# Between the layers: one weight tile's split on ScalarE and GpSimd, the next tile's split and the second block's transposes later in the order

## The chip, the cores and the metric

One core of a Trainium2 chip runs the whole program. The metric is the device time of one execution in microseconds (us), the median of several runs. A profiled execution of the kernel before gives the trace. In the text PE is TensorE (the matrix engine), DVE is VectorE, ACT is ScalarE, POOL is GpSimd and SP is the engine that issues most DMAs.

## The reference

A two-layer decoder trunk on x of 512 tokens by 1024 (float32). Layer 0 mixes tokens with native sparse attention (NSA), layer 1 with differential attention; each layer has a norm before and one after.

```python
def rmsnorm(x, g):
    y = xf * lax.rsqrt(jnp.mean(xf * xf, axis=-1, keepdims=True) + EPS)
    return (y * g.astype(jnp.float32)).astype(x.dtype)
...
    for i in range(DEPTH):                       # DEPTH = 2
        u = rmsnorm(x, norm_pre[i])
        y = nsa_mixer(u, ...) if i % 2 == 0 else diff_mixer(u, ...)   # each begins with u @ w_in, ends with o @ w_out
        x = x + rmsnorm(y, norm_post[i])
...
def diff_mixer(u, table, w_in, ...):
    q, k, v, z = jnp.split(u @ w_in, 4, axis=-1)
```

This case is about the seam: the end of `o @ w_out` of layer 0, its post-norm and the residual, the pre-norm of layer 1, and the first columns of `u @ w_in` of layer 1 (those of v).

## The kernel before, in words

Every product of a weight and an activation is made of three matmuls. Both operands are cut into a rounded part (`h`, type fp32r) and the rest (`l`), and PE adds h·h, l·h and h·l into one PSUM bank. So each weight tile of 128x1024 that a DMA brings has to be *split* before PE can use it (`Stream.split`): for each of four pieces of 128x256 one instruction writes `h` (a copy that rounds, line 158/159 or 165) and one writes `l = raw - h` (a subtraction, line 160 or 167). By default POOL does both. A table can name the engines for a tile: `"PD"` is POOL for the copy and DVE for the subtraction, `"AP"` is ACT for the copy and POOL for the subtraction.

The weight tiles form one stream, in the order in which jobs use them. A job is a set of output columns. The jobs at the seam are `o1` (columns 512 to 1023 of layer 0's output projection; 24 matmuls of 128x512 for each of the four blocks of 128 tokens, line 467), then `dv0` and `dv1` (256 columns each of layer 1's v; 24 matmuls of 128x256 a block and job, line 218). Split tiles stand in three slots `whi`/`wlo` and, at the seam alone, in six slots `wx`. `o1` has one tile in `whi`/`wlo` and three in `wx`; `dv0` has two in `whi`/`wlo`; the first tile of `dv1` stands in `wx` (it takes slots that `o1` gives up), its second in `whi`/`wlo`. DMAs fill two raw tiles `wraw` ahead of the splits.

When `o1` is done with a token block t, this chain runs for that block:

- `y_evac`: ACT squares the PSUM bank and sums (line 453), DVE multiplies it by the post-norm weight into `bigC` (line 454);
- `yend`: ACT takes a square root (line 345), DVE finishes the scale (lines 346 to 352) and writes the new x into `bigD` (line 1052, two halves of 128x512);
- `after0`: ACT issues a DMA of the block to DRAM, and `prenorm` begins: ACT squares both halves (line 361), POOL multiplies both by the pre-norm weight into `bigC` (line 364), DVE and ACT make the scale (lines 335, 345 to 349), DVE scales `bigC` (line 369);
- `turn` (called `p0` to `p3` here for the four blocks): PE transposes the block in eight matmuls (line 380), ACT copies the result as `h` into `bigF` (line 100), DVE writes `l` into `bigE` (line 105). Then `dv0` and `dv1` can use the block.

`dv0` writes block 0 and block 1 into the same PSUM bank, one half each. The second half's first matmul waits until ACT has copied the first half out (line 571). `a0` to `a3` below are the four blocks of `dv0`, `b0` to `b3` those of the first tile of `dv1`.

PE's order at the seam is the order of the code (`manual_schedule`); the list `SEQ` sets it behind `o1`. The order on the other engines comes from a list scheduler which works with its own estimates of durations; `tc.issue_after(i)` makes what is traced inside the block stand behind instruction i where they are on the same engine. The lines that matter most:

```python
            h, l = (T["wx"].tile([128, 1024], F32R, name="wx", tag="wx", bufs=6) for _ in range(2))
...
                if i in self.by:
                    eh, el = self.by[i][a // cuts]
...
    ws.by[jobs[index['dv1']].first] = SPD
```

Of the kernel before, what the change touches and what calls it, by code (L numbers as in the profile page):

```python
# [15 lines left out]
OP = mybir.AluOpType  # L16
# [2 lines left out]
S = 512  # L19
WARM = 7  # L20
EARLY = True
PRE1 = 29
ZE = 'gpsimd', 'vector'
OB = (2,2,2)
LAG = 1
# [14 lines left out]
OPRE = 0  # L40
ODELAY = 0
QN = 1
SPD = ('PD',)*4
SEQ = 'a0 a1 p2 b0 b1 a2 p3 b2 a3 b3'.split()
PRE = {16: 2, 24: 3}
SPX = ('AP',) * 4
SPN = 2
# [21 lines left out]
def trunk(ctx: ExitStack, tc: tile.TileContext, x, table, npre, npost, w_in, pe_k, w1_k, w2_k,  # L69
          pe_v, w1_v, w2_v, w_out, dw_in, lq1, lk1, lq2, lk2, subln, dw_out, steps, out):  # L70
    nc = tc.nc
# [9 lines left out]
    def bank(tag):  # L81
        return ps.tile([128, 512], F32, name=tag, tag=tag, bufs={"mm": 2, "S": 2, "T": 3, "av": 1}[tag])

    def slot(tag, shape, dt=F32):
        return big.tile(shape, dt, name="big" + tag, tag="big" + tag)
# [4 lines left out]
    def pttile(dt=F32R):  # L90
        return work.tile([128, 512], dt, name="PT", tag="PT", bufs=NPT)

    def small(n, dt=F32, tag="st", bufs=8):
        return work.tile([128, n], dt, name=tag, tag=tag, bufs=bufs)
# [4 lines left out]
    def hi(dst, src, scale=1.0):  # L99
        return nc.scalar.activation(dst, src, AF.Copy, scale=scale)  # L100
# [3 lines left out]
    def lo(dst, src, h):  # L104
        nc.vector.tensor_tensor(dst, src, h.bitcast(F32), op=OP.subtract)  # L105
# [67 lines left out]
    T = {}  # L173
# [113 lines left out]
    run = Runner()  # L287
# [43 lines left out]
    def part_sum(ss, m=EPS):  # L331

        m0 = small(1, tag="m0", bufs=6)
        if isinstance(m, float):
            nc.vector.tensor_scalar(m0, ss, 1.0 / D, m, op0=OP.mult, op1=OP.add)
        else:
            nc.vector.scalar_tensor_tensor(m0, ss, 1.0 / D, m, op0=OP.mult, op1=OP.add)
        return m0

    def row_rstd(m0, ss, split=False):  # L340

        r = small(1, tag="rstd")
        m = small(1, tag="rs1")
        q = small(1, tag="rs3")
        T0["a"] = nc.scalar.activation(r, ss, AF.Sqrt, scale=1.0 / D, bias=m0).ins
        nc.vector.scalar_tensor_tensor(m, ss, 1.0 / D, m0, op0=OP.mult, op1=OP.add)
        nc.vector.reciprocal(r, r)
        nc.vector.scalar_tensor_tensor(q, r, m, r, op0=OP.mult, op1=OP.mult)
        nc.vector.tensor_scalar(q, q, -0.5, 1.5, op0=OP.mult, op1=OP.add)
        if split:  # L350
            return r, q
        nc.vector.tensor_tensor(r, r, q, op=OP.mult)
        return r

    def prenorm(t, src, xn, grow, uh, ul, early):

        halves = (slice(0, 512), slice(512, 1024))
        ss = [small(1, tag="ss") for _ in range(2)]
        with tc.issue_after(T0["a"]) if "a" in T0 else ExitStack():
            for c, s in zip(halves, ss):  # L360
                nc.scalar.activation(pttile(F32) if early else xn[:, c], src[:, c], AF.Square, accum_out=s)
        if early:
            for c, g in zip(halves, grow):
                nc.gpsimd.tensor_tensor(xn[:, c], src[:, c], g, op=OP.mult)
        m0 = part_sum(ss[0])
        if early:
            r, q = row_rstd(m0, ss[1], split=True)
            for c in halves:
                nc.vector.tensor_scalar(xn[:, c], xn[:, c], r, q, op0=OP.mult, op1=OP.mult)
        else:  # L370
            r = row_rstd(m0, ss[1])
            for c, g in zip(halves, grow):
                nc.vector.scalar_tensor_tensor(xn[:, c], src[:, c], r, g, op0=OP.mult, op1=OP.mult)

        def turn():
            for i in range(2):
                p = bank("T")
                for j in range(4):
                    k = i * 4 + j
                    nc.tensor.transpose(p[:, j * 128:(j + 1) * 128], xn[:, k * 128:(k + 1) * 128], ident)  # L380
                pv = p.rearrange("p (j c) -> p j c", j=4)
                cs = slice(t * 128, (t + 1) * 128)
                x = hi(uh[:, i * 4:i * 4 + 4, cs], pv).ins
                T0["h"] = x
                if t == 0:
                    T0["a"] = x
                lo(ul[:, i * 4:i * 4 + 4, cs], pv, uh[:, i * 4:i * 4 + 4, cs])
        return turn
# [215 lines left out]
    index = {j.name: i for i, j in enumerate(jobs)}  # L604
    ws.extra.add(jobs[index['dv1']].first)
    ws.by[jobs[index['dv1']].first] = SPD

# [56 lines left out]
    xn = slot("D", [128, NT, D])  # L664
    for t in range(NT):
        prenorm(t, xt[:, t], xn[:, t], gpre, U["h"], U["l"], False)()
        for _ in range(8):
            run.step()
# [299 lines left out]
    for ui, u in enumerate(units):  # L968
        g = u.g
# [95 lines left out]
    def after0(t, x1, y):  # L1065
        T0.clear()
        nc.scalar.dma_start(x1d[t * 128:(t + 1) * 128, :], x1)
        if t == 0:
            U1["h"] = slot("F", [128, KD, S], F32R)
            U1["l"] = slot("E", [128, KD, S], F32R)  # L1070
        T["pre", t] = prenorm(t, x1, y, g1, U1["h"], U1["l"], EARLY)
        if t == 2:
            T["pre", 0]()
# [4 lines left out]
    T["wx"] = wx_ctx.enter_context(tc.tile_pool(name="wx", bufs=1))  # L1078
    with tc.manual_schedule(engines={mybir.EngineType.PE}):
        run.upto("oC")  # L1080
        while run.i <= index["o1"]:
            run.step()
            if run.done - T.setdefault("o1b", run.done) > PRE1 * 640:
                if ("pre", 1) in T:
                    T.pop(("pre", 1))()
        T["dv"] = slot("A", [128, NT, D])
        U["h"], U["l"] = U1["h"], U1["l"]
        ws.split()
        gens = [jobs[index[n]].run(jobs[index[n]].first) for n in ("dv0", "dv1")]
        for w in SEQ:  # L1090
            if w[0] == "p":
                T["pre", int(w[1])]()
            else:
                for _ in range({"a": 8, "b": 4}[w[0]]):
                    next(gens["ab".index(w[0])], None)
        for g in gens:
            for _ in g:
                pass
        run.i = index["dv2"]
        run.done += 2 * jobs[index["dv0"]].cost  # L1100
    wx_ctx.close()
# [169 lines left out]
```

## Time and profile before

| | us |
|---|---|
| median of 3 runs | 672.92 (671.29 to 674.07) |
| the profiled execution, its own time | 666.73 |
| its span, first to last instruction | 664.8 |

The profile page lists each engine's busy time, 40 slices of the span, the chain that ended last and the costliest groups. A view by time lists instructions with their start, their duration and, in brackets, how long the engine had been idle and what ended that. A matmul's own duration contains a pipeline delay; how fast PE goes is read from the distance of one start to the next. PEclk is the share of TensorE's clock that was granted.

### The profile page before, as it was taken

What the parts mean: (1) busy time and instruction counts of PE and PEld (TensorE: products, weight loads), DVE (VectorE), ACT (ScalarE), POOL (GpSimd) and SP (SyncE); (2) the same over time, 40 slices, a digit from 0 to 9 for tenths busy, and PEclk for the clock granted to TensorE, in tenths of its full rate; (3) what the DMA queues carried; (4) which work ended last, traced back from release to release, by engine and by line L of the source; (5) the groups of instructions that cost most, each with busy time, mean ns of one, the idle gap of its engine ahead of it and who ended that gap; (6) DMA issues with size and microseconds to landing.
All of it is one profiled execution on the core that took longest, in us unless ns stands there. A gap on an engine that the chain in (4) does not pass through costs nothing.

```text
span 664.8 us, 11267 instructions
## 1 busy us (share of the span) xinstructions
PE 638.5 (96%) x3773; PEld 555.4 (84%) x3773; DVE 434.2 (65%) x1224; ACT 340.6 (51%) x904; POOL 402.5 (61%) x675
## 2 busy tenths in 40 slices
PE   6999999999999999999999899999999999899996
PEld 5888888888788788888887899888888887779885
DVE  4611235688878878969878700147859769996834
ACT  5311234675667567778553311235455556577531
POOL 4778568777778587758487358948465464332300
PEclk8999999999999999999999899999999999999998
DMA  7565433113022121201942222323223222114402
GB/s 251 141 166 134 124 80 93 53 34 84 12 65 65 33 63 29 53 17 48 322 149 93 96 64 76 116 65 110 65 76 84 72 72 65 64 63 155 164 26 101
DMA packets 68989, 60.52 MB, mean 91 GB/s; under 512 B 3628, under 2 KB 60868, under 8 KB 68932
## 3 DMA queue, kind: packets, MB, share of 16 engines
q1 hardware_dynamic: 68212, 57.45, 29.6%
q10 hardware_dynamic: 720, 2.36, 0.9%
q8 instruction: 30, 0.49, 0.3%
q14 instruction: 27, 0.22, 0.1%
HBM read 55.04 MB, written 4.76 MB: 90 GB/s over the span
## 4 chain that ended last, share of the span: by engine, by line
PE 74%; DVE 15%; ACT 5%; issue 3%; DMA 2%; POOL 0%; SPq 0%; DVEq 0%; ACTq 0%; POOLq 0%
PE mm L198 28%; PE mm L218 10%; PE mm L467 6%; PE T L856 5%; PE av L870 5%; PE S L218 5%; PE S L801 4%; PE S L800 3%; PE S L467 3%; DVE stk L105 3%; DVE P L792 1%; PE T L721 1%; PE av L1162 1%; DMA wraw<-in_nsa_w_in_dram 1%; ACT stk L100 1%
## 5 line engine op out<-in xcount | busy, mean ns | idle before, releaser
L167 POOL TENSOR_TENSOR wlo<-wraw,whi 128x256 fp32r<-128x256 f32 (+2 forms) x247 | 185.5, 779 | 22.9 <-DVE st L792 12.1
L165 POOL TENSOR_SCALAR whi<-wraw 128x256 fp32r<-128x256 f32 (+1 forms) x240 | 95.6, 424 | 115.0 <-PE mm L198 54.9
L794 ACT ACTIVATE P<-P,st 128x512 f32<-128x512 f32 (+3 forms) x192 | 107.4, 560 | 89.2 <-DVE st L792 88.3
L850 POOL TENSOR_SCALAR P<-P,st,gate 128x512 f32<-128x512 f32 (+3 forms) x128 | 80.1, 639 | 27.3 <-DVE st L847 22.6
L198 PE MATMUL mm<-bigA,whi 128*128 128x512 f32 x192 | 77.3, 403 | 0.1
L792 DVE CUSTOM_DVE_ANT_0 P<-S,BT 128x128 f32<-128x128 f32 (+2 forms) x144 | 59.7, 418 | 24.2 <-PE S L801 21.9
L198 PE MATMUL mm<-bigB,whi 128*128 128x512 f32 x192 | 75.4, 393 | 0.0
L198 PE MATMUL mm<-bigA,wlo 128*128 128x512 f32 x192 | 75.3, 392 | 0.0
L105 DVE TENSOR_TENSOR PT<-T,PT 128x512 fp32r<-128x512 f32 x84 | 56.9, 685 | 8.2 <-ACT PT L100 6.2
L870 PE MATMUL av<-PT,bigE 128*128 128x512 f32 x160 | 56.4, 417 | 1.1 <-DVE bigF L878 0.9
L100 ACT ACTIVATE stk<-mm 64x512 fp32r<-64x512 f32 x64 | 37.9, 591 | 33.2 <-PE mm L198 17.8
L218 PE MATMUL mm<-whi,bigF 128*128 128x256 f32 x176 | 50.4, 288 | 2.3 <-DVE stk L105 2.3
L856 PE MATMUL T<-ident,P 128*128 128x128 f32 x320 | 51.7, 272 | 0.0
L100 ACT ACTIVATE PT<-T 128x512 fp32r<-128x512 f32 x84 | 48.6, 591 | 6.1 <-PE T L856 3.9
L856 PEld LDWEIGHTS T<-ident,P 128*128 128x128 f32 x320 | 41.0, 140 | 12.3 <-issue 0.4
L198 PE MATMUL mm<-bigF,whi 128*128 128x512 f32 x128 | 51.1, 399 | 0.0
L421 DVE SCALAR_TENSOR_TENSOR stk<-mm,stk 64x512 fp32r<-64x512 f32 x32 | 22.1, 690 | 44.5 <-ACT stk L100 43.7
L198 PE MATMUL mm<-bigF,wlo 128*128 128x512 f32 x128 | 50.5, 395 | 0.0
L198 PE MATMUL mm<-bigE,whi 128*128 128x512 f32 x128 | 50.2, 392 | 0.0
L218 PE MATMUL mm<-wlo,bigF 128*128 128x256 f32 x176 | 49.9, 284 | 0.0
L218 PE MATMUL mm<-whi,bigE 128*128 128x256 f32 x176 | 49.4, 283 | 0.0
L198 PEld LDWEIGHTS mm<-bigB,whi 128*128 128x128 f32 x192 | 36.0, 188 | 8.1
(286 smaller groups left out, 1675.3 us busy)
## 6 DMA issues: line engine op xcount, KB each, us to landing
wraw<-in_diff_w_in_dram SPq DMA_DIRECT2D x31, 512.0 KB, 3.8
wraw<-in_nsa_w_in_dram SPq DMA_DIRECT2D x26, 512.0 KB, 4.0
BT<-rd SPq DMA_DIRECT2D x32, 128.0 KB, 3.2
wraw<-in_diff_w_out_dram SPq DMA_DIRECT2D x5, 512.0 KB, 3.8
bigF<-in_x_dram SPq DMA_DIRECT2D x4, 512.0 KB, 9.8
wraw<-in_nsa_w_out_dram SPq DMA_DIRECT2D x4, 512.0 KB, 3.5
bigD<-in_x_dram SPq DMA_DIRECT2D x4, 512.0 KB, 4.2
x1d<-bigD ACTq DMA_DIRECT2D x4, 512.0 KB, 5.1
```

The lines of the kernel that those rows point to most:

```text
L100: return nc.scalar.activation(dst, src, AF.Copy, scale=scale)
L105: nc.vector.tensor_tensor(dst, src, h.bitcast(F32), op=OP.subtract)
L165: nc.gpsimd.tensor_scalar(h[:, a:b], v, 1.0, 0.0, op0=OP.mult, op1=OP.add)
L167: e.tensor_tensor(l[:, a:b], v, h[:, a:b].bitcast(F32), op=OP.subtract)
L198: T["mm"] = nc.tensor.matmul(p[:, a:b], wt[:, k, :], u[:, k, a:b], start=(k == 0 and j == 0), stop=(k == KD - 1 and j == 2)).ins
L218: nc.tensor.matmul(acc[t], u[:, k0 + k, t * 128:(t + 1) * 128], wt[:, k, :], start=(ci == 0 and k == 0 and j == 0 and t % per == 0), stop= ...
L467: nc.tensor.matmul(p, U[u][:, k, t * 128:(t + 1) * 128], wt[wi], start=start and j == 0, stop=stop and j == 2, skip_group_check=True)
L792: nc.vector.tensor_tensor_reduce(out=o, in0=i0, in1=b, op0=OP.add, op1=OP.min, scale=-1.0, scalar=BIG, accum_out=nm)
L794: nc.scalar.activation(pt[:, :n], pt[:, :n], AF.Exp, bias=nm, scale=-1.0, accum_out=den)
L850: NORM(nc, i, br, qb).tensor_scalar(self.P[i][:, :n], self.P[i][:, :n], st[:, 8 + i:9 + i], gate[:, NT - 1 - qb, c:c + 1], op0=OP.mult, op ...
L856: T["tmark"] = nc.tensor.transpose(p[:, j * 128:(j + 1) * 128], self.P[j][:, kb * 128:(kb + 1) * 128], ident).ins
L870: nc.tensor.matmul(av, T["V"][:, br, kb, g, :], p, start=(br == 0 and kb == 0 and j == 0), stop=(br == 1 and kb == qb and j == 1))
```

## The change

The first tile of `dv1` is split by the pairs `"AP"` in place of `"PD"`: ACT copies, POOL subtracts. `p1` is no longer called inside `o1` when a given amount of matmul work is done (`PRE1`), but first in `SEQ`, behind the whole of `o1`. Everything in `SEQ`, with the splits that the jobs `dv0` and `dv1` ask for when they end a tile, stands in an `issue_after` block behind the last pre-norm product of POOL (line 364, block 3).

```diff
-PRE1 = 29
...
-SPD = ('PD',)*4
-SEQ = 'a0 a1 p2 b0 b1 a2 p3 b2 a3 b3'.split()
+SPD = ('AP',)*4
+SEQ = 'p1 a0 a1 p2 b0 b1 a2 p3 b2 a3 b3'.split()
...
             for c, g in zip(halves, grow):
-                nc.gpsimd.tensor_tensor(xn[:, c], src[:, c], g, op=OP.mult)
+                T["xm"] = nc.gpsimd.tensor_tensor(xn[:, c], src[:, c], g, op=OP.mult).ins
...
-        while run.i <= index["o1"]:
-            run.step()
-            if run.done - T.setdefault("o1b", run.done) > PRE1 * 640:
-                if ("pre", 1) in T:
-                    T.pop(("pre", 1))()
+        run.upto("o1")
...
         gens = [jobs[index[n]].run(jobs[index[n]].first) for n in ("dv0", "dv1")]
-        for w in SEQ:
...
-        for g in gens:
-            for _ in g:
-                pass
+        with tc.issue_after(T["xm"]):
+            for w in SEQ:
...
+            for g in gens:
+                for _ in g:
+                    pass
```

Line numbers after the change are lower by one up to the seam and by four behind it. POOL at the seam: `whi`/`wlo` is the second tile of `dv1`, `wx` its first; line 364 (363 after) makes the pre-norm products, two instructions a block. Before:

```order
L167 TENSOR_TENSOR wlo<-wraw,whi 128x256 x4
L364 TENSOR_TENSOR bigC<-bigD,P 128x512 x4
L165 TENSOR_SCALAR whi<-wraw 128x256 x4
L167 TENSOR_TENSOR wlo<-wraw,whi 128x256 x2
L159 TENSOR_SCALAR wx<-P 128x256 x4
L167 TENSOR_TENSOR wlo<-wraw,whi 128x256 x2
L364 TENSOR_TENSOR bigC<-bigD,P 128x512 x4
L165 TENSOR_SCALAR whi<-wraw 128x256 x4
```

And after the change:

```order
L166 TENSOR_TENSOR wlo<-wraw,whi 128x256 x4
L363 TENSOR_TENSOR bigC<-bigD,P 128x512 x4
L159 TENSOR_TENSOR wx<-P,wx 128x256 x4
L363 TENSOR_TENSOR bigC<-bigD,P 128x512 x4
L164 TENSOR_SCALAR whi<-wraw 128x256 x4
L166 TENSOR_TENSOR wlo<-wraw,whi 128x256 x4
L164 TENSOR_SCALAR whi<-wraw 128x256 x4
```

Between the products of block 1 and those of block 2, eight instructions for the second tile and four copies of the first became four subtractions of the first; the second tile's eight stand behind the products of block 3.

ACT from the post-norm root of block 2 to the copy of the first half of the `dv0` bank (line 571, 570 after). Before:

```order
L345 ACTIVATE rstd<-ss,m_4175 128x1
L361 ACTIVATE PT,ss<-bigD 128x512
L100 ACTIVATE bigF<-T 128x4x128 x2
L1067 DMA x1d<-bigD 128x1024
L361 ACTIVATE PT,ss<-bigD 128x512
L453 ACTIVATE PT,ss<-S 128x512
L345 ACTIVATE rstd<-ss,m_4388 128x1
L345 ACTIVATE rstd<-ss,m_4187 128x1
L571 ACTIVATE bigA<-S 128x256
```

And after the change:

```order
L344 ACTIVATE rstd<-ss,m_4175 128x1
L99 ACTIVATE wx<-P 128x256 x4
L360 ACTIVATE PT,ss<-bigD 128x512
L1066 DMA x1d<-bigD 128x1024
L360 ACTIVATE PT,ss<-bigD 128x512
L452 ACTIVATE PT,ss<-S 128x512
L99 ACTIVATE bigF<-T 128x4x128 x2
L344 ACTIVATE rstd<-ss,m_4388 128x1
L344 ACTIVATE rstd<-ss,m_4187 128x1
L570 ACTIVATE bigA<-S 128x256
```

The four rounding copies came in ahead of block 2's squares, and block 1's two copies out of the transposes (`bigF<-T`) went behind block 3's `y_evac` square. On DVE the four subtractions of line 160 that stood behind block 2's line 1052 are gone, and block 3's line 454 now stands ahead of block 1's line 105. On PE the three last matmuls of `o1` stand ahead of `p1`'s eight transposes, not behind them. SP's order is the same.

## Rows read from the trace of the kernel before

**Rows 1.** From the page: each engine's busy time, share of the span, instructions.

```profile
PE 638.5 (96%) x3773; PEld 555.4 (84%) x3773; DVE 434.2 (65%) x1224; ACT 340.6 (51%) x904; POOL 402.5 (61%) x675
```

**Rows 2.** Stretches: length; PE, PEld, DVE, ACT, POOL busy (instructions); clock; DMA share, GB/s.

```profile
367.98:370.45 2.47, 0.02 (x2) 0.00 (x1) 2.47 (x6) 0.84 (x5) 0.89 (x1) 0.98 0.96 354
370.45:373.80 3.35, 3.35 (x16) 3.35 (x17) 3.35 (x15) 0.00 (x0) 0.00 (x0) 0.51 0.02 10
```

**Rows 3.** PE by time: p1, first and last of a0, a1, p2, p3.

```profile
363.18 1.25 PE L380 MATMUL T<-ident,bigC 128*128 128x128 f32 x8 [0.61 <-DVE bigC L369]
...
364.97 0.28 PE L218 MATMUL S<-whi,bigF 128*128 128x256 f32 x1
...
367.72 0.28 PE L218 MATMUL S<-whi,bigE 128*128 128x256 f32 x1
370.45 0.58 PE L218 MATMUL S<-whi,bigF 128*128 128x256 f32 x1 [2.45 <-ACT bigA L571]
...
374.87 1.04 PE L380 MATMUL T<-ident,bigC 128*128 128x128 f32 x8
...
381.45 1.03 PE L380 MATMUL T<-ident,bigC 128*128 128x128 f32 x8
```

**Rows 4.** ACT by time, blocks 1 and 2.

```profile
357.25 0.63 ACT L361 ACTIVATE PT<-bigD 128x512 f32<-128x512 f32 x1 [0.31 <-DVE m L335]
...
358.45 0.58 ACT L100 ACTIVATE bigF<-T 128x512 fp32r<-128x512 f32 x1
...
365.19 0.63 ACT L361 ACTIVATE PT<-bigD 128x512 f32<-128x512 f32 x1 [5.31 <-DVE bigD L1052]
...
365.82 1.07 ACT L100 ACTIVATE bigF<-T 128x512 fp32r<-128x512 f32 x2
...
369.65 0.48 ACT L345 ACTIVATE rstd<-ss,m 128x1 f32<-128x1 f32 x2 [1.57 <-DVE m L335]
370.04 0.36 ACT L571 ACTIVATE bigA<-S 128x256 f32<-128x256 f32 x1
```

**Rows 5.** DVE by time, blocks 1 to 3 (361.35 is the second L348).

```profile
355.43 1.42 DVE L1052 SCALAR_TENSOR_TENSOR bigD<-bigC,rstd,bigD 128x512 f32<-128x512 f32 x2
...
358.00 1.25 DVE L346 SCALAR_TENSOR_TENSOR rs<-ss,m 128x1 f32<-128x1 f32 x1 [0.88 <-ACT PT L361]
...
361.35 0.77 DVE L348 SCALAR_TENSOR_TENSOR rs<-rstd,rs 128x1 f32<-128x1 f32 x1
...
362.30 1.37 DVE L369 TENSOR_SCALAR bigC<-bigC,rstd,rs 128x512 f32<-128x512 f32 x2
...
366.23 3.26 DVE L160 TENSOR_TENSOR wx<-P,wx 128x256 fp32r<-128x256 f32 x3
369.41 0.14 DVE L335 TENSOR_SCALAR m<-ss 128x1 f32<-128x1 f32 x1
369.48 0.41 DVE L160 TENSOR_TENSOR wx<-P,wx 128x256 fp32r<-128x256 f32 x1
...
371.07 0.68 DVE L454 TENSOR_TENSOR bigC<-S,P 128x512 f32<-128x512 f32 x1
...
379.07 1.00 DVE L369 TENSOR_SCALAR bigC<-bigC,rstd,rs 128x512 f32<-128x512 f32 x2
```

**Rows 6.** POOL by time, from the second tile's split on.

```profile
360.68 1.42 POOL L167 TENSOR_TENSOR wlo<-wraw,whi 128x256 fp32r<-128x256 f32 x2
362.08 1.84 POOL L159 TENSOR_SCALAR wx<-P 128x256 fp32r<-128x256 f32 x4
...
365.72 3.15 POOL L364 TENSOR_TENSOR bigC<-bigD,P 128x512 f32<-128x512 f32 x2
...
385.43 1.51 POOL L165 TENSOR_SCALAR whi<-wraw 128x256 fp32r<-128x256 f32 x4 [8.20 <-PE S L218]
```

**Rows 7.** ACT's groups by shape: a rounding copy of 128x256 from SBUF.

```profile
L100 ACT ACTIVATE bigC<-wraw 128x256 fp32r<-128x256 f32 x6 | 2.0, 404 | 3.6 <-DMA wraw<-in_nsa_w_in_dram 3.6
```

**Rows 8.** From the page: weight loads of layer 1, KB each, us to landing.

```profile
wraw<-in_diff_w_in_dram SPq DMA_DIRECT2D x31, 512.0 KB, 3.8
```

More of the change, by code (lines that the diff above doesn't have):

```diff
@@ L1089, in trunk @@
         gens = [jobs[index[n]].run(jobs[index[n]].first) for n in ("dv0", "dv1")]
-        for w in SEQ:
[L1091 to L1095, printed above, removed]
-        for g in gens:
-            for _ in g:
-                pass
+        with tc.issue_after(T["xm"]):
+            for w in SEQ:
+                if w[0] == "p":
+                    T["pre", int(w[1])]()
+                else:
+                    for _ in range({"a": 8, "b": 4}[w[0]]):
+                        next(gens["ab".index(w[0])], None)
+            for g in gens:
+                for _ in g:
+                    pass
         run.i = index["dv2"]
```

## The prediction

> **What bounds the kernel now.** The page comes first: PE is busy for 638.5 us, 96% of the span [rows 1], and no other engine is near that. So only time in which PE stands still, or runs slowly, can be won. PE's list by time shows both at the seam, close together [rows 3]. The reader is to see three places. PE idles 0.61 us ahead of `p1`, for DVE's line 369. It idles 2.45 us ahead of `a1`, for ACT's line 571. And `a1` is slow: its 24 matmuls take from 370.45 to 374.87, 4.42 us, while `a0` starts its 24 at 364.97 and the last at 367.72, so one each 0.12 us and 2.87 in all. The stretches say why: from 370.45 to 373.80 the granted clock is 0.51, the lower level (1.2 GHz of 2.4), behind a stretch of 2.47 us in which PE did next to nothing [rows 2]. That is 4.42 - 2.87 = 1.55 us more.
>
> Why line 571 is late is read backwards. On ACT it stands behind two roots (line 345) which waited 1.57 us for DVE's line 335 [rows 4]. On DVE line 335 starts at 369.41, behind three of the four subtractions of line 160, which took 3.26 us [rows 5]. They cost so much because of POOL: the fourth, alone, took 0.41, but the three stood beside POOL's two products (365.72, 3.15 us) [rows 5, 6]. So a subtraction that nobody at the seam needs yet holds up a 0.14 us instruction on which PE waits.
>
> **The change, step by step.** I name times as in the trace before and work out where each step lands.
>
> *The copies on ACT.* Four copies of 128x256 at about 0.40 us [rows 7], overlapped some 1.4 us together. ACT had 5.31 us of idle time ahead of 365.19 [rows 4], and the `wx` slot that they fill is one that `o1`'s last block gives up near its fourth step, about 360.3. So they run from 360.3 to about 361.7 and cost nothing. If that cover were gone they would cost 1.4 us.
>
> *The subtractions on POOL.* Before, POOL had two subtractions from 360.68, 0.71 us each, then four copies (1.84), then more [rows 6]. Now the four `wx` subtractions start at about 360.74 and POOL is free at about 364.0, before block 2's products want it. What they do to DVE is the open price. Beside such a subtraction DVE's line 348, 128x1, took 0.77 us until POOL was done [rows 5, 6]: DVE waits for the whole POOL instruction. Beside POOL's copies the two line 369 took 1.37, against 1.00 alone at 379.07 [rows 5]: that looks more like a shared path. Which of the two do line 369 (block 1) and line 1052 (block 2) get now? Lower bound: as at 379.07, no delay. Upper bound: each waits for one subtraction. The new neighbours are subtractions, so I take the waiting: the first line 369 waits until 362.8 and ends at 363.3, the second waits for the fourth subtraction and ends at 364.4 (before: 363.67).
>
> A page speaks here, and against the change. The Trainium skill, "SBUF — State Buffer", section "Who interferes with whom", says that VectorE and GpSimd share a port pair under an exclusive lock, and that a VectorE instruction with two SBUF inputs or in a 2-port mode is blocked for the whole GpSimd instruction. By it the sum is 670.4; by the milder row it would be 669.4. The trace agrees for line 348 (0.77), less clearly for line 369 (1.37 for two).
>
> *DVE without them.* Line 1052 of block 2 then runs from 364.55 and, in 1.42 as at 355.43 [rows 5], ends at about 365.95 (before: when line 160 began, 366.23). Line 335 follows at once, not 3 us later.
>
> *ACT's chain up to line 571.* In block 1 the second square starts at 357.25, 0.40 after line 1052 ended at 356.85, and the copy `bigF<-T` at 358.45, 1.20 later [rows 4, 5]. Now the same chain holds block 2's square, block 3's `y_evac` and `p1`'s two copies (1.07 together at 365.82), then two roots and line 571; from the first root to PE's restart were 0.80 us (369.65 to 370.45) [rows 3, 4]. Sum: 365.95 + 0.40 + 1.20 + 0.97 + 0.80 = 369.32. `p1`'s two copies, which used to fill a wait, now stand in this chain: 0.97 of the gain goes there.
>
> *One more wait.* The third matmul of `a1` reads block 1's `bigE` (DVE, line 105). On DVE that is now behind line 346 and line 454 of block 3. Line 346 took 1.25 beside a POOL product at 358.00 [rows 5]; POOL's products of block 2 end at about 368.3 now. Then line 454 (0.68), so line 105 is done near 369.7 and PE waits 0.2. PE's effective restart: 369.5 in place of 370.45, a gain of 0.95.
>
> *`p1` behind `o1`.* The three matmuls (0.7 us) fill the 0.61 wait, but the second line 369 is later, so `p1` is done at about 365.0, as before. Gain 0. `a0` ends at 368.0 as before, and PE then idles 1.3 to 1.5 us instead of 2.45.
>
> *The clock.* At 2.45 us idle it fell. No idle time between 1.3 and 2.4 us at the seam is in the rows, so the bounds are 0 and 1.55. An idle time of 1.4 is nearer to the 0.61 ahead of `p1`, behind which `a0` ran at full pace [rows 3], so I take 1.55 as won.
>
> *The second tile's split and `p3`.* Its eight instructions were done when block 2's products began at 365.72 [rows 6]; now they stand behind block 3's products, by my estimate from 375.7 to 380. POOL's next work began at 385.43 [rows 6], now 2.5 earlier, and PE wants the tile about then. Cover: 3 us. Its raw buffer comes free 14 us later, so SP issues one load 14 us later, and that lands 3.8 us on [rows 8], at about 384. The tile it brings is split behind eight instructions that begin at 383, of 0.40 to 0.71 each: 2 to 3 us to spare. Block 3's line 369 ended at 380.07, 1.38 ahead of `p3` at 381.45 [rows 3, 5]. `p3` comes 2.5 earlier, DVE's chain by my estimate about 1.5 to 2, one wait for a subtraction included. It is just covered; without that it costs up to 1 us.
>
> **Sum.** 0.95 + 1.55 = 2.5 us. Behind the seam the order is unchanged and PE is the bound [rows 1], so the gain is carried to the end: 666.73 - 2.5 = 664.2 for a profiled execution. The runs' median lies 6.19 above the profiled time, 672.92; the same 2.5 off it gives 670.4.
>
> **Rivals.**
> 1. *DVE is hardly held by the subtractions* (the 1.37 at 362.30 speaks for it, the 0.77 at 361.35 against). Line 369 ends at 363.3, line 1052 at 364.9, line 571's chain restarts PE at 368.3, with the 0.2 wait 368.5. Gain 1.95 + 1.55 = 3.5: 669.4. Chance 0.17.
> 2. *The wait moves and the clock falls all the same*: PE still idles some 1.4 us, then 0.2, behind `p1` with two short waits. Or the runs before fell less than the profiled one. Then only 0.95 is won: 672.0. Chance 0.20.
> 3. *Slower: the second tile's split gets in `p3`'s way.* Block 3's lines 346, 348 and twice 369 each need two SBUF inputs or run as line 369 did; if each waits for a POOL instruction of 0.73 that is 2.9, against 1 us of cover: PE loses 1.9 at `p3`, and with PE idle that long the clock falls, another 1.55. Net 2.5 - 3.45: about 1 us slower, 673.9. It decides when block 3's second line 369 ends over 2.5 us behind the end of `a2`. That line 160 cost 3.26 in the same company speaks for it; that PE is at the transposes for 0.4 before it needs the second half, against. Chance 0.08.
> 4. *The copies come late* (the `wx` slot given up later than I read) and nothing is won at line 571: 672.9. Chance 0.05.
>
> **The numbers.** My forecast has 0.50. A measurement of this kernel can tell about 0.5%, 3.4 us, from no change, and the forecast of 2.5 lies within it. Faster by more: most of rival 1 and the upper end of the forecast, 0.20. Slower by more needs rival 3 with a second loss behind it or a drift of the runs: 0.07. Within: 0.73. The runs before lie 1.6 below to 1.2 above their median. The range goes from rival 1 less 1.4 to rival 2 plus 1.4: 668.0 to 673.4; the forecast's own is 669.2 to 671.6.
>
> **What would show it.** Right: ACT's four `wx` copies between 360 and 362, POOL's four subtractions right behind, line 335 of block 2 within 0.5 us of line 1052, an idle time ahead of `a1` of 1.2 to 1.6, and a granted clock near 1.00 in `a1`. Wrong: a stretch near 0.5 behind that wait (rival 2), line 1052 of block 2 ended by 365 (rival 1), or idle time ahead of `p3` (rival 3). What would make me most wrong is a new wait behind the seam that these rows do not hold.

## The result, and the profile after

The changed kernel took **668.78 us** (median of 10 runs, 665.03 to 670.43) beside 672.78 for the kernel before (10 runs, 670.55 to 674.58): a ratio of **0.9937, 95% interval 0.9915 to 0.9959**. Forecast were 670.4, a gain of 2.5, and a range of 668.0 to 673.4; measured is a gain of 4.0. On another chip (run e7 below) the ratio was 0.9973, 0.9952 to 0.9995. Both intervals lie below 1, so it is faster; that it is faster by more than 0.5% is not shown.

The page of the changed kernel, busy time of each engine (its profiled execution took 670.43 us, its span is 668.5):

```profile
PE 640.8 (96%) x3773; PEld 556.7 (83%) x3773; DVE 436.7 (65%) x1220; ACT 342.3 (51%) x908; POOL 404.3 (60%) x675
```

Nothing is to be read from that against [rows 1]: PE is the bound as before. The span is even 3.7 us longer than that of the profiled execution before, which took 6 us less than the median of its kernel, while the medians say the opposite. Two executions differ in many places; the seam has to be compared by itself. PE by time in the changed kernel (`p0`, the two halves of `p1`, the first of `a0`, the first four of `a1`, `p2`, `p3`):

```profile
359.45 1.03 PE L379 MATMUL T<-ident,bigC 128*128 128x128 f32 x8
...
366.06 0.66 PE L379 MATMUL T<-ident,bigC 128*128 128x128 f32 x4
367.02 0.63 PE L379 MATMUL T<-ident,bigC 128*128 128x128 f32 x4 [0.30 <-DVE rstd L351]
367.40 0.36 PE L217 MATMUL S<-whi,bigF 128*128 128x256 f32 x1
...
371.76 0.39 PE L217 MATMUL S<-whi,bigF 128*128 128x256 f32 x1 [1.24 <-ACT bigA L570]
371.98 0.28 PE L217 MATMUL S<-wlo,bigF 128*128 128x256 f32 x1
372.14 0.39 PE L217 MATMUL S<-whi,bigE 128*128 128x256 f32 x1
372.37 0.28 PE L217 MATMUL S<-whi,bigF 128*128 128x256 f32 x1
...
374.86 1.04 PE L379 MATMUL T<-ident,bigC 128*128 128x128 f32 x8
...
381.45 1.03 PE L379 MATMUL T<-ident,bigC 128*128 128x128 f32 x8
```

And `p0` in the kernel before:

```profile
356.67 1.03 PE L380 MATMUL T<-ident,bigC 128*128 128x128 f32 x8
```

This execution comes to the seam 2.78 us later than the one before, yet `p2` and `p3` start at the same times [rows 3]. So the seam is 2.8 us shorter. From `a0` to `a1` it is 4.36 us in place of 5.48; from `a1` to `p2` 3.10 in place of 4.42. Stretches of the changed kernel (columns as in [rows 2]): the wait, `a1`.

```profile
370.36:371.76 1.40, 0.16 (x2) 0.00 (x1) 1.40 (x4) 1.35 (x5) 0.44 (x1) 1.00 0.13 50
371.76:374.86 3.10, 3.10 (x24) 3.02 (x25) 3.06 (x12) 0.00 (x0) 0.00 (x0) 1.00 0.00 0
```

The granted clock is 1.00 in `a1`, where it was 0.51 [rows 2]. DVE by time (line 368 of block 1, block 2's lines 1051 and 334, and at the end block 3's line 368):

```profile
365.22 1.66 DVE L368 TENSOR_SCALAR bigC<-bigC,rstd,rs 128x512 f32<-128x512 f32 x2
...
366.98 1.42 DVE L1051 SCALAR_TENSOR_TENSOR bigD<-bigC,rstd,bigD 128x512 f32<-128x512 f32 x2
368.52 0.15 DVE L334 TENSOR_SCALAR m<-ss 128x1 f32<-128x1 f32 x1
...
379.65 1.94 DVE L368 TENSOR_SCALAR bigC<-bigC,rstd,rs 128x512 f32<-128x512 f32 x2
```

Line 334 follows line 1051 at once; before, 3 us of line 160 stood between [rows 5]. Line 1051 itself takes 1.42. POOL by time (the first tile's subtractions, the second tile's split, the next split), then ACT (the `wx` copies, `p1`'s two copies):

```profile
363.60 2.99 POOL L159 TENSOR_TENSOR wx<-P,wx 128x256 fp32r<-128x256 f32 x4 [1.61 <-ACT wx L99]
...
378.21 1.51 POOL L164 TENSOR_SCALAR whi<-wraw 128x256 fp32r<-128x256 f32 x4
379.69 3.19 POOL L166 TENSOR_TENSOR wlo<-wraw,whi 128x256 fp32r<-128x256 f32 x4
385.43 1.52 POOL L164 TENSOR_SCALAR whi<-wraw 128x256 fp32r<-128x256 f32 x4 [2.55 <-PE S L217]
```

```profile
363.10 1.34 ACT L99 ACTIVATE wx<-P 128x256 fp32r<-128x256 f32 x4 [0.47 <-issue]
...
370.00 1.07 ACT L99 ACTIVATE bigF<-T 128x512 fp32r<-128x512 f32 x2
```

### The profile page after: what moved, and what is told of

Its sections match the earlier page's. It is cut to its first block, busy times and chain, and to the rows that moved or that the text cites. A ratio compares the mean times of both kernels' runs of the same rounds, so it can differ in the third digit from the quotient of the medians.

```text
span 668.5 us, 11268 instructions
## 1 busy us (share of the span) xinstructions
PE 640.8 (96%) x3773; PEld 556.7 (83%) x3773; DVE 436.7 (65%) x1220; ACT 342.3 (51%) x908; POOL 404.3 (60%) x675
## 4 chain that ended last, share of the span: by engine, by line
PE 75%; DVE 14%; ACT 4%; issue 2%; DMA 2%; POOL 1%; SPq 0%; DVEq 0%; ACTq 0%; POOLq 0%
PE mm L197 29%; PE mm L217 10%; PE mm L466 6%; PE av L869 5%; PE T L855 5%; PE S L217 4%; PE S L800 4%; PE S L799 4%; PE S L466 3%; DVE stk L104 2%; PE av L1158 1%; PE T L720 1%; DVE P L791 1%; DMA wraw<-in_nsa_w_in_dram 1%; DMA P<-in_diff_w_in_dram 1%
```

## The experiments

The change has three parts: the pairs of `SPD`, the `issue_after` block (the *tie*), and `p1` behind `o1`. My theory (1) was that the first carries the gain, by the shorter wait ahead of `a1` and the clock that stays; the rival (2) that the tie and the later `p1` carry it. To compare traces, one number is used: the length of the *seam*, from one matmul of layer 0 (the last line 800 `S<-bigC,stk` behind a wait of 0.54 or 0.55 us) to one of layer 1 (the first line 218 `mm<-whi,bigF` behind a wait of 0.45 or 0.46). In the kernel before it is 433.36 - 306.31 = 127.05 us. All runs:

| run | `SPD` | tie | `p1` | seam, us | wait ahead of `a1` | median, us | ratio to before (95%) |
|---|---|---|---|---|---|---|---|
| before | PD | no | in `o1` | 127.05 | 2.45 | | |
| changed | AP | yes | behind | 124.32 | 1.24 | 668.78 | 0.9937 (0.9915, 0.9959) |
| e1 | AP | no | in `o1` | 127.00 | 1.09 | 670.62 | 1.001 (0.999, 1.0029) |
| e2 | PD | yes | behind | 123.36 | 1.21 | 666.37 | 0.995 (0.9931, 0.9969) |
| e3 | AP | no | behind | 127.19 | 2.70 | 670.23 | 1.0007 (0.9991, 1.0023) |
| e4 | AP | yes | in `o1` | 124.02 | 0.47 | 666.94 | 0.9953 (0.9931, 0.9975) |
| e5 | PD | yes | in `o1` | 123.45 | 0.78 | 666.53 | 0.9952 (0.9935, 0.997) |
| e6 | no subtractions | no | in `o1` | 124.01 | 0.76 | 666.41 | 0.9956 (0.9938, 0.9975) |
| e7, changed again | AP | yes | behind | 124.27 | 1.25 | 666.28 | 0.9973 (0.9952, 0.9995) |
| e8, before again | PD | no | in `o1` | 127.12 | 2.45 | 669.01 | 0.9996 (0.9977, 1.0016) |

For e1 to e4 the kernel before had a median of 670.17 on the same chip, for e5 to e8 670.08. The medians in the first four expectations were worked out from 672.8, so it is the distance to before that counts.

**e1, the pairs alone.**

```diff
-SPD = ('PD',)*4
+SPD = ('AP',)*4
```

> The kernel before with SPD as 'AP' and nothing else: p1 stays inside o1, there is no issue_after block. POOL keeps the second tile's eight instructions between the products of block 1 and block 2, with the four subtractions of the first tile among them. Theory 1 (the gain comes from taking line 160 out from between line 1052 and line 335 of block 2, that is the shorter wait ahead of a1 and the clock that does not fall): line 335 of block 2 starts within 0.5 us of line 1052, the idle time ahead of a1 is 1.0 to 1.6 us, the granted clock in a1 is near 1.00; POOL has 12 instructions where it had 12, but four copies of 0.46 are now subtractions of 0.71, so block 2's products begin about 1 us later, which p2 does not see. Gain 2.5 to 3.5 us at the seam, median 669 to 670. Theory 2 (the tie and the later p1 carry the gain): line 335 still comes late or p2 waits, gain under 1 us, median 672 to 673.

No gain: theory 1 fell. The trace (by time: DVE's line 1052 of block 2, block 3's line 1052, block 2's line 369; POOL's products of blocks 2 and 3; PE at `a1` and `p2`):

```profile
367.46 2.34 DVE L1052 SCALAR_TENSOR_TENSOR bigD<-bigC,rstd,bigD 128x512 f32<-128x512 f32 x2
...
373.76 1.42 DVE L1052 SCALAR_TENSOR_TENSOR bigD<-bigC,rstd,bigD 128x512 f32<-128x512 f32 x2
375.10 2.90 DVE L369 TENSOR_SCALAR bigC<-bigC,rstd,rs 128x512 f32<-128x512 f32 x2
...
370.37 2.51 POOL L364 TENSOR_TENSOR bigC<-bigD,P 128x512 f32<-128x512 f32 x2
374.60 3.12 POOL L364 TENSOR_TENSOR bigC<-bigD,P 128x512 f32<-128x512 f32 x2 [1.72 <-DVE bigD L1052]
...
372.25 0.38 PE L218 MATMUL S<-whi,bigF 128*128 128x256 f32 x1 [1.09 <-ACT bigA L571]
...
376.74 0.63 PE L380 MATMUL T<-ident,bigC 128*128 128x128 f32 x4 [1.35 <-DVE bigC L369]
378.14 0.63 PE L380 MATMUL T<-ident,bigC 128*128 128x128 f32 x4 [0.78 <-DVE m L335]
```

At `a1` all came as expected: line 335 follows line 1052 at once (369.72), the wait is 1.09, and the clock does not fall (1.00 in `a1`). It was given back at `p2`, 2.13 us. POOL has twelve instructions in front of block 2's products, as before, but four of them are now subtractions, and the products end at 372.88, 13.3 us behind the start of `p0` where it was 12.2; block 2's line 369 comes behind block 3's line 1052, and then beside block 3's products, 2.90 us for two where two take 1.00 alone [rows 5].

**e2, all but the pairs.** The changed kernel with

```diff
-SPD = ('AP',)*4
+SPD = ('PD',)*4
```

> The changed kernel with SPD back at 'PD': DVE makes the four subtractions again, now ahead of line 1052 of block 2, POOL makes the four copies, p1 is behind o1 and the issue_after block stands. Theory 1: the subtractions take 0.41 each when POOL is not in company and up to 1.05 where it is, 1.6 to 4.2 us on DVE's chain to line 335, so line 335 comes 1.5 to 4 us later than in the changed kernel, PE idles 2 us or more ahead of a1 and the clock falls there; gain against before 0 to 1.5 us, median 671.5 to 673.5. Theory 2 (the tie and the later p1 carry the gain): as the changed kernel, 668 to 670.

Theory 2's number came, and more. DVE by time, the subtractions and line 1051 of block 2:

```profile
363.81 0.42 DVE L159 TENSOR_TENSOR wx<-P,wx 128x256 fp32r<-128x256 f32 x1
...
364.21 1.10 DVE L159 TENSOR_TENSOR wx<-P,wx 128x256 fp32r<-128x256 f32 x3
365.22 1.41 DVE L1051 SCALAR_TENSOR_TENSOR bigD<-bigC,rstd,bigD 128x512 f32<-128x512 f32 x2
```

The four subtractions cost DVE 1.5 us in place of 3.7 [rows 5]. They now stand ahead of line 1051, where POOL is idle, and no longer behind it beside block 2's products. So my lower price, 0.41 each, is the one that holds.

**e3, no tie.** The changed kernel with

```diff
-        with tc.issue_after(T["xm"]):
+        if True:
```

> The changed kernel without the issue_after block: the second tile's eight instructions stand ahead of block 2's products on POOL again, twelve instructions of 0.45 to 0.73 between the products of block 1 and block 2. Theory 1: DVE's line 348, 369 and 1052 meet POOL in any case, so the wait ahead of a1 is as in the changed kernel or up to 0.5 us longer; block 2's products begin about 3 us later than in the changed kernel (near 366.3 in the time of the trace before), so p2, which needs line 369 of block 2, may come up to 0.5 us later. Median 668.8 to 669.8. Theory 2 (the tie is needed): p2 waits for line 369 by 1 us or more, median 670.5 to 672.

The whole gain went, though not where theory 2 had it: `p2` waits little, `a1` waits longest of all. DVE and PE by time, and the stretch of `a1`:

```profile
364.52 2.34 DVE L1051 SCALAR_TENSOR_TENSOR bigD<-bigC,rstd,bigD 128x512 f32<-128x512 f32 x2
...
370.23 0.58 PE L217 MATMUL S<-whi,bigF 128*128 128x256 f32 x1 [2.70 <-ACT bigA L570]
```

```profile
370.23:373.60 3.37, 3.37 (x16) 3.37 (x17) 3.33 (x12) 0.43 (x1) 0.38 (x1) 0.53 0.00 0
```

Line 1051 takes 2.34 again beside POOL's subtractions, `p1`'s copies stand in ACT's chain, and the lower clock (0.53) comes behind the wait.

**e4, `p1` back in `o1`.** The changed kernel with

```diff
+PRE1 = 29
-SEQ = 'p1 a0 a1 p2 b0 b1 a2 p3 b2 a3 b3'.split()
+SEQ = 'a0 a1 p2 b0 b1 a2 p3 b2 a3 b3'.split()
-        run.upto("o1")
+        while run.i <= index["o1"]:
...
```

> The changed kernel with p1 back inside o1, three matmuls ahead of its end; SPD stays 'AP' and the issue_after block stands. Theory 1: p1's two copies (0.97 us) fill a wait on ACT again and leave the chain to line 571, and line 105 of block 1 stands ahead of line 346 and 454 of block 3 on DVE, so PE restarts at a1 about 0.9 us earlier and the 0.2 us wait in a1 is gone; against that p1 waits inside o1 for the second line 369, 0.6 us before and up to 1.3 now, where the three matmuls (0.7 us) no longer fill it. Net 0 to 0.7 us better than the changed kernel, median 668.1 to 668.8. Theory 2 (the later p1 is a part of the gain): 0.7 us or more worse than the changed kernel, 669.5 or more.

PE by time, `p1` and `a1`:

```profile
364.69 0.66 PE L380 MATMUL T<-ident,bigC 128*128 128x128 f32 x4 [0.71 <-DVE bigC L369]
365.65 0.63 PE L380 MATMUL T<-ident,bigC 128*128 128x128 f32 x4 [0.31 <-DVE rstd L352]
...
370.32 0.38 PE L218 MATMUL S<-whi,bigF 128*128 128x256 f32 x1 [0.47 <-ACT bigA L571]
```

As theory 1 had it: `a1` waits 0.77 less, `p1` 0.72 more, and the seam is 0.30 shorter. The later `p1` is no part of the gain.

**e5, the tie alone.** The kernel before, with `T["xm"]` and the `issue_after` block of the change, and nothing else of it. By now two theories were left: that of company (A), and that the tie needs another part (B).

> The kernel before with the issue_after block alone: SPD stays 'PD', p1 stays inside o1. The first four runs left two theories. Theory A (company): the seam is slow because POOL's eight instructions for the second tile run beside DVE's chain of block 2; line 1052 of block 2 took 2.35 us for its two halves beside POOL's subtractions (before, SPD alone, no tie) and 1.42 where POOL was idle (changed kernel, tie with 'PD', p1 in o1). Then the tie alone gives all of it: line 1052 of block 2 takes 1.4, the four subtractions of line 160 near 0.4 each, the idle time ahead of a1 is 0.8 to 1.3, the clock stays near 1.00, median 3.4 to 4.2 us below the kernel before. Theory B (the tie needs the later p1 or the moved subtractions with it): gain under 2 us.

DVE by time, the subtractions and line 1052 of block 2; POOL, the four copies and block 2's products; then PE:

```profile
363.04 0.42 DVE L160 TENSOR_TENSOR wx<-P,wx 128x256 fp32r<-128x256 f32 x1
...
363.44 1.09 DVE L160 TENSOR_TENSOR wx<-P,wx 128x256 fp32r<-128x256 f32 x3
364.44 1.42 DVE L1052 SCALAR_TENSOR_TENSOR bigD<-bigC,rstd,bigD 128x512 f32<-128x512 f32 x2
...
360.42 1.52 POOL L159 TENSOR_SCALAR wx<-P 128x256 fp32r<-128x256 f32 x4 [1.12 <-PE S L467]
365.28 2.97 POOL L364 TENSOR_TENSOR bigC<-bigD,P 128x512 f32<-128x512 f32 x2 [3.34 <-DVE bigD L1052]
...
368.25 0.39 PE L218 MATMUL S<-whi,bigF 128*128 128x256 f32 x1 [0.78 <-ACT bigA L571]
```

Theory A's number came: the tie alone makes the seam 3.60 us shorter (0.9952 in time), and here `p1` does not wait at all. But the theory names only a part of the way. The tie does two things. No instruction of the second tile runs beside line 1052 any more (1.42 in place of 2.35). And the four copies of the first tile no longer queue behind the second tile's instructions: they end at 361.94, before at 363.92 [rows 6], so the subtractions come ahead of line 1052, in a stretch of 3.34 us in which POOL is idle, where before three of them stood beside block 2's products. No run does one of the two without the other.

**e6, no subtractions.** The kernel before, but for the four subtractions of `dv1`'s first tile ACT writes the rounded piece once more:

```diff
-SPD = ('PD',)*4
+SPD = ('PX',)*4
...
+                    if el == "X":
+                        hi(l[:, a:b], v)
+                        continue
```

> The kernel before without the four subtractions of line 160: ACT writes the rounded piece once more in their place (four more copies in its idle time), so the low part of that one tile is not the remainder. POOL's order is that of before, the second tile's split among it. This is the upper bound of what moving the subtractions off DVE can give without a cost elsewhere. Theory A: line 1052 of block 2 still takes 2.35 beside POOL's subtractions and ends near 366.2 in the time of the trace before, line 335 follows at once, ACT's chain to line 571 ends near 368.4, PE idles 0.9 to 1.2 us ahead of a1 and the clock stays; block 2's products begin at 365.7 as before and take 2.98, so p2 does not wait: 2.5 to 3.2 us below before. Theory C (the subtractions never were what a1 waits for): a1 idles 2 us or more, no gain.

DVE by time, line 1052 and 335 of block 2 (lines are higher by three):

```profile
364.70 2.35 DVE L1055 SCALAR_TENSOR_TENSOR bigD<-bigC,rstd,bigD 128x512 f32<-128x512 f32 x2
366.98 0.14 DVE L338 TENSOR_SCALAR m<-ss 128x1 f32<-128x1 f32 x1
```

As theory A had it: line 1052 still takes 2.35, but line 335 follows at once, the seam is 3.04 us shorter. So the subtractions were on the path to `a1`, and theory C is out. Either works by itself, the tie (e5) or DVE without the subtractions (e6, which leaves them out and is no kernel to keep). What does not work is to move them to a POOL that is still full (e1, e3).

**e7 and e8, both kernels once more**, unchanged.

> The changed kernel once more, on the same chip as the two above, so that it can be set beside them. Theory A and the seam of its trace (2.7 us shorter from a fixed matmul of layer 0 to a fixed one of layer 1): 2.4 to 3.2 us below before. Rival: 4.0 us below as in the first ten runs, then 1.3 us more come from places which the first trace does not show.

> The kernel before once more, for a second trace and the granted clock of each of its runs. If the lower clock behind the 2.45 us wait ahead of a1 is there in this trace too, it belongs to the seam and not to one execution; its time should not differ from the runs of before by more than 0.2%, and its seam, from a fixed matmul of layer 0 to a fixed one of layer 1, should be 127.0 us long, within 0.3. Rival: a seam without the fall, 125.5, in which case the 1.55 us are won in some runs only.

PE by time in e8, the two ends of the seam and `a1`, then a stretch of `a1`:

```profile
305.79 0.37 PE L800 MATMUL S<-bigC,stk 128*128 128x288 f32 x1 [0.54 <-DVE st L792]
...
369.95 0.47 PE L218 MATMUL S<-whi,bigF 128*128 128x256 f32 x1 [2.45 <-ACT bigA L571]
...
432.91 0.36 PE L218 MATMUL mm<-whi,bigF 128*128 128x256 f32 x1 [0.45 <-DVE stk L105]
```

```profile
369.95:373.30 3.35, 3.35 (x16) 3.35 (x17) 3.35 (x15) 0.00 (x0) 0.00 (x0) 0.52 0.03 11
```

The wait and the fall belong to the seam of the kernel before, not to one execution (127.12 and 127.05 us). The changed kernel's seam repeats as well (124.27 and 124.32): 2.73 to 2.85 us shorter, which is 0.9958 to 0.9959 of the time before and lies within both intervals, just. The medians, 4.0 and 3.8 apart, say more; e7's ratio of 0.9973, which is not the quotient of its two medians (0.9943), says less. So e7 does not decide between its two expectations, and that more than the seam is won is not shown.

## Why the prediction was right, and what in it was wrong

**The number.** Forecast was a gain of 2.5, the seam gives 2.8. The 4.0 between the medians holds 1.2 us more, of which no trace shows the place. Taking 2.78 us off the times after, step by step:

- *Copies on ACT*: start 363.10 - 2.78 = 360.3, as forecast, and hidden.
- *Subtractions on POOL and line 369 of block 1*: POOL from 360.82 to 363.8 (forecast 360.74 to 364.0). DVE was held, nearer to the waiting bound than to the other: its two line 368 take 1.66 in place of 1.00 and end at 364.1 (forecast 364.4, without a delay 363.3). Rival 1 is out: line 1051 ended at 365.6, not by 365. The Trainium skill, "SBUF — State Buffer", section "Who interferes with whom", has whichever of VectorE and GpSimd comes second fully blocked for the other's whole instruction, where the two contend. The trace agrees where block 2's line 369 stood beside products of about 1.5 us in e1 (2.90 for two, against 1.00 alone); beside shorter subtractions, of 0.75 each, the price was smaller, 1.66. POOL is held as well: its two subtractions beside line 1052 took 1.87 in the kernel before, where the two ahead of the copies took 1.42 [rows 6].
- *ACT's chain*: line 1051 ended at 365.62. With the forecast's 0.40 + 1.20 + 0.97 + 0.80 PE should restart at 368.99; it did at 368.98.
- *One more wait*: the third and fourth matmul of `a1` start 0.16 and 0.23 behind the one ahead instead of 0.12, so 0.15 are lost (forecast 0.2).
- *`p1`*: forecast 0, measured 0.35: from `p0` to `a0` 7.95 us in place of 8.30. This term was too low.
- *The clock*: 1.55 forecast. `a1` takes 3.10 in place of 4.42, and with the 0.15 of the wait the pace alone gives 1.47. Rival 2 is out, in both traces.
- *Second tile and `p3`*: split from 378.21 to 382.88, that is 375.4 to 380.1 (forecast 375.7 to 380). Block 3's line 368 is held, 1.94 for two, and ends at 381.59, when `p3` has begun its first half at 381.45 without a wait. POOL idles 2.55 ahead of its next split at 385.43. So the cover held, by little.

**The reason.** The step that failed is the one from the cause to the edit. The cause is "So a subtraction that nobody at the seam needs yet holds up a 0.14 us instruction on which PE waits." That is true of the rows, and e6 confirms it (3.04 us). But moving those subtractions to POOL is not what wins: alone this leaves the seam at 127.00 us (e1), and with the tie it costs 0.6 to 1.0 (changed against e2: 124.32 and 123.36; e4 against e5: 124.02 and 123.45). The tie carries the gain. I had entered it only as a risk for `p3`, at a price of nothing. Its effect was hidden in another term: "in 1.42 as at 355.43" for line 1052. In the trace of before that line took 2.35 for block 2, beside POOL's two subtractions (`wlo`), and I took the duration from block 1, where POOL stood idle until block 1's own products began (356.26):

```profile
363.96 2.35 DVE L1052 SCALAR_TENSOR_TENSOR bigD<-bigC,rstd,bigD 128x512 f32<-128x512 f32 x2
...
363.89 1.87 POOL L167 TENSOR_TENSOR wlo<-wraw,whi 128x256 fp32r<-128x256 f32 x2
```

The prediction did have POOL free from 364.0, but does not say that this is the tie's doing. The 1.42 is right only because the tie takes POOL's eight instructions away (1.41 or 1.42 in the changed kernel, e2, e4 and e5, 2.34 or 2.35 in e1, e3 and e6).

So the prediction has the right time by the right places with the credit on the wrong edit. My expectation for e1, from the same reasons, was 2.5 to 3.5 us and wrong by all of it, because it did not follow POOL's queue on to block 2's products and `p2`.

**A better version.** The tie alone (e5) and the tie with the later `p1` (e2) have the shortest seams, 0.8 to 1.0 us below the changed kernel. In time that is not told apart: 666.53 and 666.28 for e5 and the changed kernel on one chip.

## What to carry to other kernels

Cost a queue in the company that it will keep: the same two instructions of DVE took 1.0 or 2.9 us together, depending on what POOL did, so the duration has to be taken from a row with the same neighbour. Before work is moved to a second engine, follow that engine's queue to the next thing on which the bound waits; putting off work that nobody needs yet can do more than moving it. And run each part of a composite change alone: the sum can be right with the shares wrong.

## What the runs showed of the hardware

The granted clock is not a function of the wait ahead alone. Late in layer 1 PE stands behind the same wait of 1.31 us in the changed kernel and in its repetition e7. One stretch ends where the wait ends, the other begins 0.9 us later (in between the granted clock was 0.95 and 1.00). First of the changed kernel:

```profile
574.00:577.69 3.69, 1.97 (x13) 1.24 (x11) 3.65 (x8) 1.00 (x4) 2.58 (x4) 1.00 0.01 3
578.60:581.90 3.30, 3.30 (x13) 2.82 (x12) 2.86 (x6) 1.66 (x4) 0.00 (x0) 0.50 0.29 109
```

and of e7:

```profile
568.46:572.15 3.69, 1.97 (x12) 1.25 (x11) 3.65 (x8) 1.00 (x4) 2.58 (x4) 1.00 0.00 0
573.10:576.40 3.30, 3.30 (x21) 2.75 (x20) 3.22 (x7) 2.00 (x5) 0.00 (x0) 1.00 0.32 122
```

PE was busy for 1.97 of the 3.69 us in both, and the clock went to its lower level (0.50) in one and stayed at 1.00 in the other; 13 instructions came through in the 3.30 us where 21 did. At the seam, the three traces with a wait of 2.45 to 2.70 us have the lower level behind it, the seven with 0.47 to 1.25 have not. What decides the cases between stays open here; it may be a part of why executions of one kernel lie some 5 us apart (of e7's twelve runs the fastest, 663.82 us, had a mean granted clock of 0.996, the slowest, 671.28 us, of 0.988).
